# Two of the four weight sums of a seven-product pair: from VectorE to accumulating transfers issued by GpSimd

## The chip, the cores and the metric

The kernel runs on one core of one Trainium2 chip. The metric is the device time of one execution in microseconds. Before the change it is 2252.79 us, the median of three runs (2252.79 to 2252.91).

## What is computed

The reference is a trunk of two layers over 256 tokens of width 2048, all in float32. Each layer normalises its input, projects it by `w_in` (2048 x 6144), runs two kinds of attention, projects by `w_o` (2048 x 2048), adds the normalised result, and then runs a gated feed-forward block, which is where the change is:

```python
def swiglu(h, w_gate, w_up, w_down):
    return (jax.nn.silu(h @ w_gate) * (h @ w_up)) @ w_down
...
        h = rms_norm(x, pre_ffn_norm[l])
        f = swiglu(h, w_gate[l], w_up[l], w_down[l])
        x = x + rms_norm(f, post_ffn_norm[l])
```

`w_gate` and `w_up` are 2048 x 5632, `w_down` is 5632 x 2048.

## The kernel before

**Weights as a stream.** All weights are cut into blocks of 256 rows by 512 columns (512 KB), and `queue_pair` (line 96) lists the blocks in the order in which they are used. A block is held as a tile `raw` of 128 partitions by 2 by 512; the index 0 or 1 in the middle says which 128 rows. `fetch` (line 136) allocates the tile (four buffers) and issues its load on SyncE's queue (SP, line 140). `feed` (line 167) splits each block into two float32r parts: ScalarE makes `hi` (line 177), VectorE the rest `lo` (line 179), six buffers each. `weights(i, ahead)` (line 187) feeds the stream up to four blocks beyond the one that is asked for. TensorE forms each product as three matmuls: hi by hi, hi by lo, lo by hi.

**Gate and up.** A column chunk c (eleven per layer, 512 columns each) needs eight blocks of `w_gate` and eight of `w_up`, one of each per pair kp. Four PSUM banks collect the two token halves by gate and up. An ordinary pair (`eight`, line 726) makes eight products, 24 matmuls. The pairs kp 2, 4 and 6 (`SEVEN`; only 4 and 6 in a layer's first chunk, where the order is `FIRST_ORDER`) make seven products, 21 matmuls, by a Strassen-like scheme over the 2 x 2 blocks: token halves by row blocks, row blocks by gate or up (`seven`, line 736). It needs four sums of weight blocks. With g the gate block and u the up block they are t1 = g0 + u0, t3 = u0 + u1, t2 = t1 + u1 and t4 = t2 + g1. `mixed_weights` (line 145) makes them: four additions on VectorE (line 151) into two tiles T (t1 and t3 in one, t2 and t4 in the other), then the split of u1 (lines 155 and 156) and of the two T tiles into Th (ScalarE, line 160) and Tl (VectorE, line 162). The block g itself takes the ordinary split. There are 32 such pairs per layer, 64 in all. After the last pair of a chunk the extra products are combined in four tiles w (lines 778 to 783, tag `t2`), and lines 788 to 791 apply the gate.

**Order.** The program is traced in the order of the code. A scheduler then orders each engine's instructions by its own model of when they are ready, with the traced order as priority; each engine's queue then runs strictly in that order, and an instruction that waits holds up all behind it. Tiles with the same tag share a fixed number of buffers, and the first writer of a tile waits for the last reader of the buffer's former tile. At a few places the order is given by hand. One is `in_turn` (line 183), which holds a small load behind the latest block's load. Another is the end of the output projection (lines 676 to 687), where `feed` and `fetch` are called with explicit indices while ScalarE and VectorE keep the traced order; there the stream's index `idx + 4` is the first gate block of the layer.

Of the kernel before, what the change touches and what calls it, by code (L numbers as in the profile page):

```python
# [9 lines left out]
F32 = mybir.dt.float32  # L10
# [3 lines left out]
ALU = mybir.AluOpType  # L14
# [3 lines left out]
P = 128  # L18
# [7 lines left out]
CW = 512  # L26
# [25 lines left out]
def kernel(  # L52
# [21 lines left out]
    nc = tc.nc  # L74
# [19 lines left out]
    stream = []  # L94
# [8 lines left out]
    sevens = set()  # L103
# [29 lines left out]
    raws, loads = [], []  # L133
    fed = [0]

    def fetch(upto):
        while len(raws) < min(upto, len(stream)):
            i = len(raws)
            raw = wpool.tile([P, 2, CW], F32, tag="raw", bufs=4, name=f"raw{i}")
            loads.append(nc.sync.dma_start(raw, stream[i]))  # L140
            raws.append(raw)

    mix_pool = [None]

    def mixed_weights(i):

        g, u = raws[i - 1], raws[i]
        sums = [mix_pool[0].tile([P, 2, CW], F32, tag="T", bufs=2, name=f"T{i}_{j}") for j in range(2)]
        t1, t3, t2, t4 = sums[0][:, 0, :], sums[0][:, 1, :], sums[1][:, 0, :], sums[1][:, 1, :]
        for o, a, b in ((t1, g[:, 0, :], u[:, 0, :]), (t3, u[:, 0, :], u[:, 1, :]), (t2, t1, u[:, 1, :]), (t4, t2, g[:, 1, :])):  # L150
            nc.vector.tensor_tensor(out=o, in0=a, in1=b, op=ALU.add)  # L151
        parts = []
        hi = wpool.tile([P, 2, CW], F32R, tag="hi", bufs=6, name=f"hi{i}")
        lo = wpool.tile([P, 2, CW], F32R, tag="lo", bufs=6, name=f"lo{i}")
        nc.scalar.activation(hi[:, 1, :], u[:, 1, :], AF.Copy)
        nc.vector.tensor_tensor(out=lo[:, 1, :], in0=u[:, 1, :], in1=hi[:, 1, :].bitcast(F32), op=ALU.subtract)
        parts.append((hi[:, 1, :], lo[:, 1, :]))
        for j in range(2):
            th = mix_pool[0].tile([P, 2, CW], F32R, tag="Th", bufs=3, name=f"Th{i}_{j}")
            nc.scalar.activation(th, sums[j], AF.Copy)  # L160
            tl = mix_pool[0].tile([P, 2, CW], F32R, tag="Tl", bufs=3, name=f"Tl{i}_{j}")
            nc.vector.tensor_tensor(out=tl, in0=sums[j], in1=th.bitcast(F32), op=ALU.subtract)  # L162
            parts += [(th[:, k, :], tl[:, k, :]) for k in range(2)]
        b22, t1, t3, t2, t4 = parts
        return {"b22": b22, "t1": t1, "t2": t2, "t3": t3, "t4": t4}

    def feed(upto):
        fetch(upto)
        while fed[0] < min(upto, len(stream)):
            i = fed[0]  # L170
            raw = raws[i]
            if i in sevens:
                ready[i] = mixed_weights(i)
                fed[0] += 1
                continue
            hi = wpool.tile([P, 2, CW], F32R, tag="hi", bufs=6, name=f"hi{i}")
            nc.scalar.activation(hi, raw, AF.Copy)  # L177
            lo = wpool.tile([P, 2, CW], F32R, tag="lo", bufs=6, name=f"lo{i}")
            nc.vector.tensor_tensor(out=lo, in0=raw, in1=hi.bitcast(F32), op=ALU.subtract)  # L179
            ready[i] = (hi, lo)  # L180
            fed[0] += 1
# [27 lines left out]
    nc.sync.dma_start(rows0, pre_mix_norm.rearrange("l (k p) -> (l k) p", p=P))  # L209
    load_x(0, 0)  # L210
    fetch(1)
    load_x(1, 0)
    fetch(2)
    load_x(0, 1)
    fetch(3)
# [75 lines left out]
    def transposed(t, g0, tiles, cols=range(4)):  # L291
        for cg in cols:
            pb = bank(f"xT_ps{t}_{cg}")
            for j in range(4):
                k = cg * 4 + j
                nc.tensor.transpose(pb[:, j * P : (j + 1) * P], xs[t][:, k * P : (k + 1) * P], ident)
            for j in range(4):
                k = cg * 4 + j
                rounded = nc.scalar.activation(
                    tiles[k][:, 0, t * P : (t + 1) * P], pb[:, j * P : (j + 1) * P], AF.Copy, scale=gains[:, g0 + k : g0 + k + 1]  # L300
                )
            for j in range(4):
                k = cg * 4 + j
                rest = nc.vector.scalar_tensor_tensor(
                    out=tiles[k][:, 1, t * P : (t + 1) * P],
                    in0=pb[:, j * P : (j + 1) * P],
                    scalar=gains[:, g0 + k : g0 + k + 1],
                    in1=tiles[k][:, 0, t * P : (t + 1) * P].bitcast(F32),
                    op0=ALU.mult,
                    op1=ALU.subtract,  # L310
                )
        return rounded, rest
# [36 lines left out]
    def unit(accs, stat, i, kp, toks, first, last, ahead=LOOKAHEAD):  # L349
        hi, lo = weights(i, ahead)  # L350
        for kk in range(2):
            tick()
            k = 2 * kp + kk
            for t in toks:
                st = stat[k]
                sh, sl = st[:, 0, t * P : (t + 1) * P], st[:, 1, t * P : (t + 1) * P]
                a = accs[t]
                nc.tensor.matmul(a, sh, hi[:, kk, :], start=first and kk == 0, stop=False)  # L358
                nc.tensor.matmul(a, sh, lo[:, kk, :], start=False, stop=False)  # L359
                nc.tensor.matmul(a, sl, hi[:, kk, :], start=False, stop=last and kk == 1)  # L360


    def evac_chunk(pool, acc, mg, ssm, gpost, c, t, nm, mpool=None):
        junk = pool.tile([P, CW], F32, tag="t2", name=f"jm_{nm}_{t}_{c}")
        nc.scalar.activation(junk, acc, AF.Square, accum_out=ssm[t][:, c : c + 1])
        if c % 2 == 0:
            mg[t, c // 2] = (mpool or pool).tile([P, 2, CW], F32, tag="qk", bufs=4, name=f"mg_{nm}_{t}_{c}")
        m = mg[t, c // 2][:, c % 2, :]
        nc.vector.tensor_tensor(out=m, in0=acc, in1=gpost[:, c * CW : (c + 1) * CW], op=ALU.mult)

    def rescale(mg, ssm, t, nm, then=None):
        tot = small.tile([P, 2], F32, tag="tot", name=f"tot_{nm}_{t}")
        nc.vector.tensor_reduce(out=tot[:, 0:1], in_=ssm[t], axis=AX.X, op=ALU.add)
        rsqrt(tot[:, 1:2], tot[:, 0:1], 1.0 / D, f"{nm}_{t}_p")
        for c in range(4):
            sl = xs[t][:, c * CW : (c + 1) * CW]
            nc.vector.scalar_tensor_tensor(
                out=sl, in0=mg[t, c // 2][:, c % 2, :], scalar=tot[:, 1:2], in1=sl, op0=ALU.mult, op1=ALU.add
            )
            if then is not None:  # L380
                then(t, c)
# [266 lines left out]
    for l in range(L):  # L648

        pool = tc.alloc_tile_pool(name=f"att{l}", bufs=6, reuse_waits="tile")  # L650
# [25 lines left out]
        idx = plan[l]["o"][3, 4]  # L676
        with tc.manual_schedule(engines={mybir.EngineType.Activation, mybir.EngineType.DVE}):
            feed(idx + 6)
            for kp in range(4, 8):
                unit(accs, mix, idx + kp - 4, kp, (0,), False, kp == 7, 0)  # L680
            evac_chunk(pool, accs[0], mg, ssm, gpost, 3, 0, f"o{l}")
            rescale(mg, ssm, 0, f"o{l}")
            for kp in range(4, 8):
                feed(idx + 3 + kp)
                fetch(idx + 8 + kp)
                unit(accs, mix, idx + kp - 4, kp, (1,), False, kp == 7, 0)
                transposed(0, 32 + l * KT, xT, cols=(kp - 4,))
        with tc.high_priority(offset=URGENT):
# [3 lines left out]
        pool.release()  # L692


        pool = tc.alloc_tile_pool(name=f"ffn{l}", bufs=6, reuse_waits="tile")
        gu = tc.alloc_tile_pool(name=f"gu{l}", bufs=1, reuse_waits="tile")
        mix_pool[0] = gu
        act = []
# [213 lines left out]
```

## Time and profile before

| | |
|---|---|
| median of three runs | 2252.79 us |
| the profiled execution | 2252.42 us |
| its span, first to last instruction | 2250.7 us |
| granted TensorE clock, mean | 0.998 |
| bytes read from HBM | 417.68 MB, 187 GB/s over the span |
| DMA share of the SP queue | 58.2% of 16 engines |
| the gate and up stage of layer 0 and layer 1 | from about 408 and 1520 us, for about 466 and 472 us |

A profile is one execution. Busy time is the time in which an engine's instructions run; the share is against the span. PE is TensorE's matmuls, PEld its weight loads, DVE VectorE, ACT ScalarE, POOL GpSimd, SP SyncE. A wait row names the instruction that waited and what ended its wait, then the total in us, how often, and the longest. In a timeline row the first number is the start and the second the duration. DVE instructions of one kind overlap a little: their durations are longer than the distance from start to start, and a sum over many is better taken from the starts.

### The profile page before, as it was taken

The page shows a single profiled execution, that of the slowest core. Times are in us where ns is not written, and L with a number is a line of the kernel's source. Part 1 is how long each engine was busy: PE and PEld are TensorE (multiplying, and loading weights), DVE is VectorE, ACT ScalarE, POOL GpSimd, SP SyncE. Part 2 cuts the span into 40 slices and gives each one's busy share as a digit, 9 for nine tenths or more (in the row PEclk, how much of TensorE's full clock was granted, in tenths as well). Part 3 has the DMA queues.
Part 4 walks back from the last instruction along what each step waited for, and adds up shares of the span by engine and source line. Part 5 has one row for each costly group of instructions (what it writes and reads, how often), then busy time and mean ns, then how long its engine had stood idle before and what let it go on. Part 6 is the DMA issues. An engine that isn't in the chain of part 4 may idle for free.

```text
span 2250.7 us, 28018 instructions
## 1 busy us (share of the span) xinstructions
PE 2225.4 (99%) x10210; PEld 1833.5 (81%) x10210; DVE 1626.3 (72%) x2225; ACT 1222.4 (54%) x1834; POOL 37.6 (2%) x76
## 2 busy tenths in 40 slices
PE   8999999999999999999999999999999999999998
PEld 6888888788888888888887888887888888888886
DVE  6666555899989988555576665559998998975555
ACT  6545555665555546444465555546655555554443
POOL 1010000000000000000010000000000000000000
PEclk9999999999999999999999999999999999999999
DMA  7555555475665666556565555554666566565553
GB/s 238 180 169 163 163 182 184 127 229 187 204 206 188 199 209 208 189 188 204 171 195 175 162 167 161 186 186 141 205 200 209 190 199 205 190 218 192 191 198 135
DMA packets 216699, 421.62 MB, mean 187 GB/s; under 512 B 13200, under 2 KB 13808, under 8 KB 216048
## 3 DMA queue, kind: packets, MB, share of 16 engines
q1 hardware_dynamic: 216560, 419.83, 58.2%
q8 instruction: 80, 1.31, 0.2%
q14 instruction: 59, 0.48, 0.1%
HBM read 417.68 MB, written 2.10 MB: 187 GB/s over the span
## 4 chain that ended last, share of the span: by engine, by line
PE 92%; DVE 3%; ACT 2%; DMA 2%; issue 0%; POOL 0%; SPq 0%; DVEq 0%; ACTq 0%
PE c L722 10%; PE c L723 10%; PE c L724 10%; PE in L358 8%; PE in L360 7%; PE in L359 7%; PE dn L843 7%; PE dn L840 7%; PE dn L841 7%; PE o L360 2%; PE o L358 2%; PE o L359 2%; PE p L724 2%; PE p L723 2%; PE p L722 2%; DVE lo L179 1%
## 5 line engine op out<-in xcount | busy, mean ns | idle before, releaser
L179 DVE TENSOR_TENSOR lo<-raw,hi 128x1024 fp32r<-128x1024 f32 x720 | 873.6, 1227 | 329.8 <-ACT hi L177 324.5
L177 ACT ACTIVATE hi<-raw 128x1024 fp32r<-128x1024 f32 x720 | 749.5, 1056 | 469.1 <-PE in L360 166.5
L722 PE MATMUL c<-hi,xF 128*128 128x512 f32 x960 | 377.8, 394 | 2.0 <-DVE w L783 1.6
L724 PE MATMUL c<-hi,xF 128*128 128x512 f32 x960 | 374.2, 391 | 0.0
L723 PE MATMUL c<-lo,xF 128*128 128x512 f32 x960 | 373.6, 390 | 0.0
L840 PE MATMUL dn<-hi,jh 128*128 128x512 f32 x656 | 255.6, 390 | 0.0
L841 PE MATMUL dn<-lo,jh 128*128 128x512 f32 x656 | 255.2, 389 | 0.0
L722 PEld LDWEIGHTS c<-hi,xF 128*128 128x128 f32 x960 | 180.6, 188 | 39.1 <-DVE w L783 2.5
L724 PEld LDWEIGHTS c<-hi,xF 128*128 128x128 f32 x960 | 180.4, 188 | 37.8
L723 PEld LDWEIGHTS c<-lo,xF 128*128 128x128 f32 x960 | 180.5, 188 | 36.3
L843 PE MATMUL dn<-hi,jl 128*128 128x512 f32 x656 | 202.1, 389 | 0.0
L160 ACT ACTIVATE Th<-T 128x1024 fp32r<-128x1024 f32 x128 | 135.2, 1056 | 116.9 <-DVE T L151 106.5
L822 DVE TENSOR_TENSOR jl<-act,jh 128x512 fp32r<-128x512 f32 x88 | 60.7, 692 | 161.6 <-ACT jh L820 159.3
L820 ACT ACTIVATE jh<-act 128x512 fp32r<-128x512 f32 x88 | 55.0, 631 | 219.3 <-PE dn L841 213.5
L162 DVE TENSOR_TENSOR Tl<-T,Th 128x1024 fp32r<-128x1024 f32 x128 | 156.2, 1220 | 1.0 <-ACT Th L160 0.3
L358 PE MATMUL in<-hi,xT 128*128 128x512 f32 x384 | 155.3, 405 | 1.3 <-ACT hi L177 1.3
L358 PE MATMUL in<-hi,xI 128*128 128x512 f32 x384 | 154.0, 401 | 0.0
L359 PE MATMUL in<-lo,xT 128*128 128x512 f32 x384 | 150.7, 392 | 0.6 <-DVE lo L179 0.6
L360 PE MATMUL in<-hi,xT 128*128 128x512 f32 x384 | 150.8, 393 | 0.0
L359 PE MATMUL in<-lo,xI 128*128 128x512 f32 x384 | 149.9, 390 | 0.3 <-DVE lo L179 0.3
L360 PE MATMUL in<-hi,xI 128*128 128x512 f32 x384 | 150.2, 391 | 0.0
L841 PEld LDWEIGHTS dn<-lo,jh 128*128 128x128 f32 x656 | 123.1, 188 | 25.6
(247 smaller groups left out, 3224.0 us busy)
## 6 DMA issues: line engine op xcount, KB each, us to landing
raw<-in_w_in_dram SPq DMA_DIRECT2D x192, 512.0 KB, 3.8
raw<-in_w_gate_dram SPq DMA_DIRECT2D x176, 512.0 KB, 3.9
raw<-in_w_up_dram SPq DMA_DIRECT2D x176, 512.0 KB, 4.5
raw<-in_w_down_dram SPq DMA_DIRECT2D x176, 512.0 KB, 4.3
raw<-in_w_o_dram SPq DMA_DIRECT2D x64, 512.0 KB, 4.1
x<-in_x_dram SPq DMA_DIRECT2D x4, 512.0 KB, 7.6
gpost_mix<-in_post_mix_norm_dram SPq DMA_DIRECT2D x2, 1024.0 KB, 7.8
gpost_ffn<-in_post_ffn_norm_dram SPq DMA_DIRECT2D x2, 1024.0 KB, 7.2
```

Source lines behind the costliest of these rows:

```text
L162: nc.vector.tensor_tensor(out=tl, in0=sums[j], in1=th.bitcast(F32), op=ALU.subtract)
L177: nc.scalar.activation(hi, raw, AF.Copy)
L179: nc.vector.tensor_tensor(out=lo, in0=raw, in1=hi.bitcast(F32), op=ALU.subtract)
L358: nc.tensor.matmul(a, sh, hi[:, kk, :], start=first and kk == 0, stop=False)
L359: nc.tensor.matmul(a, sh, lo[:, kk, :], start=False, stop=False)
L360: nc.tensor.matmul(a, sl, hi[:, kk, :], start=False, stop=last and kk == 1)
L722: nc.tensor.matmul(a, sh, hi, start=first, stop=False)
L723: nc.tensor.matmul(a, sh, lo, start=False, stop=False)
L724: nc.tensor.matmul(a, sl, hi, start=False, stop=last)
L840: nc.tensor.matmul(accs[c, t], sh, hi[:, kk, :], start=first, stop=False)
L841: nc.tensor.matmul(accs[c, t], sh, lo[:, kk, :], start=False, stop=False)
L843: nc.tensor.matmul(accs[c, t], sl, hi[:, kk, :], start=False, stop=last)
```

## The change

For the up block of a seven-product pair `fetch` loads only the half u1 into `raw`. A new helper allocates a tile Ta (two buffers), copies g0 and u1 from HBM into its halves by two more loads on SP's queue, and then issues on GpSimd's queue one transfer that reads u0 twice and adds it to both halves in SBUF. Ta then holds t1 and t3. `mixed_weights` takes Ta in place of its first T tile and adds only t2 and t4 on VectorE; T has one buffer instead of two. To make room, the feed-forward pool's tiles of tag `t2` get five buffers instead of six. The clamp on `fetch` at the end of the output projection keeps the first seven-product pair's block from being fetched before the pool that holds Ta exists.

```diff
@@ fetch
-            loads.append(nc.sync.dma_start(raw, stream[i]))
+            if i in sevens:
+                loads.append(nc.sync.dma_start(raw[:, 1, :], stream[i][:, 1, :]))
+                add_in_memory(i)
+            else:
+                loads.append(nc.sync.dma_start(raw, stream[i]))
             raws.append(raw)
 
     mix_pool = [None]
 
+    added = {}
+
+    def add_in_memory(i):
+
+        t = mix_pool[0].tile([P, 2, CW], F32, tag="Ta", bufs=2, name=f"Ta{i}")
+        nc.sync.dma_start(t[:, 0, :], stream[i - 1][:, 0, :])
+        nc.sync.dma_start(t[:, 1, :], stream[i][:, 1, :])
+        nc.gpsimd.dma_start(t, stream[i][:, 0:1, :].to_broadcast([P, 2, CW]), accum_op=ALU.add)
+        added[i] = t
+
     def mixed_weights(i):
 
         g, u = raws[i - 1], raws[i]
-        sums = [mix_pool[0].tile([P, 2, CW], F32, tag="T", bufs=2, name=f"T{i}_{j}") for j in range(2)]
+        sums = [added[i], mix_pool[0].tile([P, 2, CW], F32, tag="T", bufs=1, name=f"T{i}")]
         t1, t3, t2, t4 = sums[0][:, 0, :], sums[0][:, 1, :], sums[1][:, 0, :], sums[1][:, 1, :]
-        for o, a, b in ((t1, g[:, 0, :], u[:, 0, :]), (t3, u[:, 0, :], u[:, 1, :]), (t2, t1, u[:, 1, :]), (t4, t2, g[:, 1, :])):
+        for o, a, b in ((t2, t1, u[:, 1, :]), (t4, t2, g[:, 1, :])):
             nc.vector.tensor_tensor(out=o, in0=a, in1=b, op=ALU.add)
@@ the end of the output projection
-                fetch(idx + 8 + kp)
+                fetch(min(idx + 8 + kp, idx + 12))
@@ the feed-forward stage
-        pool = tc.alloc_tile_pool(name=f"ffn{l}", bufs=6, reuse_waits="tile")
+        pool = tc.alloc_tile_pool(name=f"ffn{l}", bufs=5, reuse_waits="tile")
```

## Prediction

> **What bounds the kernel now.** I read the engine line of the page first, then windows over the gate/up stage, then PE's waits and the chain of waits inside it.
>
> ```profile
> PE 2225.4 (99%) x10210; PEld 1833.5 (81%) x10210; DVE 1626.3 (72%) x2225; ACT 1222.4 (54%) x1834; POOL 37.6 (2%) x76
> ```
> ```profile
> 408.00:470.00 62.00, 57.73 (x260) 45.89 (x259) 57.35 (x121) 43.74 (x88) 0.00 (x0) 0.97 0.50 153
> 470.00:875.00 405.00, 405.00 (x1827) 335.59 (x1825) 362.93 (x425) 225.68 (x260) 0.00 (x0) 1.00 0.62 201
> 1520.00:1590.00 70.00, 66.45 (x299) 52.73 (x299) 65.14 (x136) 48.69 (x97) 0.00 (x0) 0.98 0.45 142
> 1590.00:1992.00 402.00, 402.00 (x1810) 332.97 (x1809) 357.78 (x418) 223.42 (x256) 0.00 (x0) 1.00 0.63 203
> ```
> ```profile
> 492.00:534.00 42.00, 42.00 (x191) 34.81 (x190) 40.47 (x47) 24.22 (x28) 0.00 (x0) 1.00 0.66 218
> ```
>
> The columns are the stretch, its length, busy time of PE, PEld, DVE, ACT and POOL, the granted clock, the DMA share and GB/s. PE has no idle microsecond in the 405 and 402 us that hold nearly all seven-product pairs. One column chunk (191 PE instructions: five eight-product pairs of 24 matmuls, three seven-product pairs of 21, eight transposes) takes 42.0 us. DVE is busy but is not what ends last. Only where a layer's gate/up stage begins does PE stand idle: 62.00 - 57.73 = 4.3 us in layer 0 and 70.00 - 66.45 = 3.6 us in layer 1. Work taken from VectorE can be repaid in those 7.9 us only; a loss has no such cap.
>
> ```profile
> PE p L723 <- DVE lo L179: 1.8, 1, 1.8
> PE q L722 <- ACT Th L160: 1.1, 1, 1.1
> PE c L722 <- DVE w L783: 0.8, 1, 0.8
> ```
> ```profile
> 429.55 4.92 DMA raw<-in_w_up_dram
> ...
> 439.40 1.20 DVE T L151 x2
> ...
> 442.48 4.02 DMA raw<-in_w_gate_dram
> ...
> 448.82 1.89 DVE T L151 x3
> ...
> 456.52 4.95 DMA raw<-in_w_up_dram
> ```
>
> These are PE's waits in 408 to 470 us (total, times, longest) and the chain there (start, length). The chain alternates between weight loads of 4 to 5 us and weight sums of 0.6 us each. Sums stand before two of the three waits (Th, and the w of line 783), not before the one for the gate pair's lo.
>
> **The sums that go.** Two of four sums per pair leave VectorE.
>
> ```profile
> L151 DVE TENSOR_TENSOR T<-raw,raw 128x512 f32<-128x512 f32 x64 | 44.2, 691 | 8.7 <-DMA raw<-in_w_up_dram 6.7
> L151 DVE TENSOR_TENSOR T<-raw 128x512 f32<-128x512 f32 x64 | 43.9, 685 | 0.0
> ```
>
> That is 88.1 us of DVE's 1626. In steady chunks it buys nothing, since PE is full there. The first chunk of a layer has two such pairs, so four sums, which follow each other at 0.60 us (below), leave its chain: at most 2.4 us a layer, 4.8 us in all.
>
> **The transfers that come.** Per pair the SP queue loses half of the up load (256 KB) and gets two copies of 256 KB; POOL gets one accumulating transfer that reads 256 KB twice and adds it into 512 KB of SBUF. No row of before shows an accumulating transfer or a DMA issued by POOL. The nearest rows:
>
> ```profile
> raw<-in_w_up_dram SPq DMA_DIRECT2D x176, 512.0 KB, 4.5
> ...
> gpost_ffn<-in_post_ffn_norm_dram SPq DMA_DIRECT2D x2, 1024.0 KB, 7.2
> out_dram<-x SPq DMA_DIRECT2D x8, 256.0 KB, 2.3
> ```
>
> The two copies should land in between 2.3 us (256 KB) and 4.5 us (512 KB); nearest is 4.5, the same bytes. The accumulate moves 512 KB and reads its destination besides: from 4.5 us (as a plain load) to 7.2 us (twice the bytes). I take 6, in the middle. From free buffer to finished sum that is 2.3 + 4.5 = 6.8 at the low end, 4.5 + 7.2 = 11.7 at the high end, 10.5 taken; the second copy's issue on SP (0.37 us, row below) and POOL's own issue, for which no row exists and which I put at the same 0.37, make it 11.2, and 7.5 to 12.4 at the ends. POOL is idle in these stages, so nothing queues behind its waits.
>
> **Who waits for the new sum.** The rows are one steady chunk, on DVE, then SP, then PE.
>
> ```profile
> 672.77 0.69 DVE L151 TENSOR_TENSOR T<-raw,raw 128x512 f32<-128x512 f32 x1
> 673.38 0.68 DVE L788 TENSOR_TENSOR w<-c,w 128x512 f32<-128x512 f32 x1
> ...
> 678.29 0.69 DVE L151 TENSOR_TENSOR T<-raw 128x512 f32<-128x512 f32 x1
> 678.89 0.69 DVE L151 TENSOR_TENSOR T<-T,raw 128x512 f32<-128x512 f32 x1
> 679.49 0.69 DVE L156 TENSOR_TENSOR lo<-raw,hi 128x512 fp32r<-128x512 f32 x1
> 680.09 0.69 DVE L151 TENSOR_TENSOR T<-T,raw 128x512 f32<-128x512 f32 x1
> 680.69 1.22 DVE L162 TENSOR_TENSOR Tl<-T,Th 128x1024 fp32r<-128x1024 f32 x1
> 681.83 1.22 DVE L179 TENSOR_TENSOR lo<-raw,hi 128x1024 fp32r<-128x1024 f32 x1
> ...
> 685.44 0.69 DVE L151 TENSOR_TENSOR T<-raw,raw 128x512 f32<-128x512 f32 x1
> ...
> 695.61 1.42 DVE L151 TENSOR_TENSOR T<-T,raw 128x512 f32<-128x512 f32 x2
> ```
> ```profile
> 680.81 0.37 SPq L140 DMA_DIRECT2D raw<-in_w_up_dram  x1
> ```
> ```profile
> 688.28 0.39 PE L722 MATMUL q<-Th,sh 128*128 128x512 f32 x1
> ...
> 698.48 0.39 PE L722 MATMUL q<-Th,sh 128*128 128x512 f32 x1
> ```
>
> The pairs are kp 2 (sums 672.77 to 680.7), kp 4 (from 685.44) and kp 6 (t2 at 695.61). After the change DVE's add for t2 waits for the accumulate, and behind it in DVE's queue stand the lo splits of the next weights, for which PE waits in the end. Cover: PE takes the first kp 2 sum at 688.28, its Tl ended at 680.69 + 1.22 = 681.9, so 6.4 us of lead.
>
> The wait's length depends on **where SP has the two copies**. Of the two Ta buffers, the one for kp 6 is that of kp 2, free when kp 2's Tl ends: 681.9. Its sum is needed at 695.61. That leaves 13.7 us, or 11.3 if DVE, four sums lighter by then, is 2.4 us earlier; my 11.2 just fits, and 12.4 would cost DVE 1.1 us out of the lead. Kp 2 and kp 4 have longer: their buffers are those of the chunk before. This holds if the copies are issued when their buffer is free and not in the traced order, behind the half load of line 140, which waits for its own buffer. Two rows speak for it: the sum at 672.77 runs ahead of line 788, which is traced before it, and
>
> ```profile
> 0.97 0.20 POOL L246 MEMSET negones<- 128x128 f32 x1
> ```
>
> runs at 0.97 us though it is traced behind a whole column chunk. What is ready early is put early in its queue. So I cost the copies and the accumulate at nothing in steady chunks.
>
> **The DMA engines** are the other cover. At a share of 0.62 the 405 us hold 405 / 42 = 9.6 chunks of 16 loads, so a 512 KB load takes 0.62 x 405 / 154 = 1.63 us of all engines. A chunk after the change has 16 - 3 x 0.5 + 3 x 1 = 17.5 such units and three accumulates of a units each. With a = 1 that is 33.4 us of the 42.0, with a = 2 38.3, with a = 3 43.2. I take 2, one read more per byte written, so the engines are 91% busy and loads will land later than now.
>
> The Trainium skill, Collectives: The Full Stack, section "The bandwidth ceiling: the fold count and why AG ≠ RS ≠ AR", says that an add in the transfer path goes at about half the rate of a copy, because it reads two sources; no run here shows one yet, and by it a would be 1.9 and the chunk's DMA work 38.0 us. The Trainium skill, DMA: Bandwidth & Descriptors, section "Anatomy of one DMA — SWDGE (gpsimd) path", puts a GpSimd transfer at 2.0 us and its bytes at 436 GB/s, an estimate of 3.2 us for 512 KB where I take 6; the sum would be the same, since both fit.
>
> **Small parts.** T keeps one buffer: its next writer (t2 of kp 4, after 685.44) comes after kp 2's second Tl (about 683 to 684.2). Five t2 buffers instead of six: the four w of a chunk are 42 us apart from the next four. The clamped fetch shortens only the traced order; loads wait for their four buffers in any case. All three at 0; without that cover each is one 0.6 to 1.2 us wait per pair or chunk.
>
> **Sum.** The profiled execution took 2252.42 us (span 2250.7 and 1.7 around it), 0.37 below the median of 2252.79. Steady chunks: 0. Each layer's start: 0 to -2.4 from the sums, against later loads on the same chain; I take -0.7 net. 2252.42 - 1.4 = **2251.0 us**. From the full gain of 4.8 to equal loss, its own range is 2247.6 to 2257. A measurement of this kernel can tell about 0.2%, 4.5 us.
>
> **Rivals.**
> *Contention at 91% share (slower).* Two pairs at a layer's start bring 2 x (0.5 + 2) = 5 units, 8.2 us of DMA work, onto a chain with three load waits (4.92, 4.02, 4.95). Half of it there is +4 a layer, all of it +8: 2252.4 + 8 to 16. Steady chunks lose too if every landing grows by one accumulate (3.3 us), which is half of the 6.4 us lead: decisive once twice that falls on one pair. About 2265, up to 2290. Against it: the share is only 0.50 at the start.
> *Copies behind the half load (slower).* Then the sum comes L = 4.6 (680.81 to 685.44) + 6 + 0.7 for issues = 11.3 us after the up buffer is free. A turn from kp 2 to kp 4 is L + 1.8 (t2, t4, half lo) against PE's 698.48 - 688.28 = 10.2; from kp 6 to the next chunk's kp 2 it is L + 1.8 + six splits of 1.14 (680.69 to 681.83) = L + 8.6. Together 3L + 12.2 against 42.0: it decides from L = 9.9; at 11.3 a chunk takes 46.1, and 20 chunks cost 82: 2334. Up to L = 12.5: 2408. Against it: the early issues above.
> *DMA bound (slower).* From a = 2.8. With a = 3, 20 x 1.2 = 24 us: 2276; with a = 4, 48.1 a chunk: 2374. Nothing in before shows a.
> *Faster.* The whole 4.8 us and no later loads: 2247.6, just past the bound. For it: sums before two of three waits. Against: 1.1 + 0.8 us of those waits per layer.
>
> **Chances.** Hidden 0.46, contention 0.24, copies behind 0.12, DMA bound 0.12, faster by over 0.2% 0.06. So same 0.46, slower 0.48. The likeliest single case is the first, 2251.0. The range 2248 to 2340 takes in it, contention, the lower half of "DMA bound" and of "copies behind"; some 0.17 stays outside.
>
> **What would show it.** Right: DVE about 88 us lighter, PE at 42.0 us a chunk with no waits in 470 to 875, the Ta copies issued more than 10 us before their t2 add, a DMA share near 0.9 there, the accumulate landing in 4.5 to 7.2 us. Wrong: DVE's t2 adds waiting on the accumulate for microseconds, Ta issues right behind their half load, a share of 1, or PE's waits at the layer starts above 4.3 and 3.6 us.

## The result and the profile after

| | before | after |
|---|---|---|
| median, 11 runs each on one chip | 2252.79 us (2250.37 to 2253.2) | 2259.23 us (2255.61 to 2265.07) |
| ratio, 95% interval | | 1.0029 (1.0021 to 1.0037) |
| the profiled execution, its span | 2252.42, 2250.7 us | 2265.07, 2263.2 us |

The kernel became slower by 0.29%, 6.4 us between the medians. The profiled execution after is the longest of its eleven, so its trace shows the loss enlarged: 12.65 us against the profiled execution before.

The page after, engines, queues and DMA issues:

```profile
PE 2230.4 (99%) x10210; PEld 1834.3 (81%) x10210; DVE 1553.1 (69%) x2097; ACT 1224.2 (54%) x1834; POOL 115.5 (5%) x140
...
q0 software_dynamic: 17408, 33.56, 8.6%
...
L156 POOL DMA_DIRECT2D Ta<-in_w_up_dram x64 | 77.9, 1218 | 1347.7 <-DVE ssx_ffn L337 284.6
...
raw<-in_w_up_dram SPq DMA_DIRECT2D x112, 512.0 KB, 5.7
Ta<-in_w_up_dram POOLq DMA_DIRECT2D x64, 512.0 KB, 8.2
...
Ta<-in_w_gate_dram SPq DMA_DIRECT2D x64, 256.0 KB, 4.1
```

VectorE has 128 instructions less and is 73.2 us lighter. The accumulating transfer lands 8.2 us behind its issue in the median, and POOL is busy 1.22 us with each issue. A plain load of an up block now lands in 5.7 us instead of 4.5.

PE's waits over the whole execution, the rows of the gate and up stages (total, times, longest), after:

```profile
PE c L736 <- DVE w L797: 6.4, 4, 2.9
...
PE p L736 <- ACT Th L174: 2.3, 2, 1.3
PE c L736 <- ACT hi L191: 2.3, 3, 1.7
```

The first row was, before,

```profile
PE c L722 <- DVE w L783: 1.6, 2, 0.8
```

and it is now the largest of the stages. The windows (same columns as in the prediction) say where:

```profile
408.00:450.00 42.00, 38.13 (x169) 29.77 (x169) 38.23 (x98) 29.35 (x73) 2.68 (x3) 0.96 0.60 167
...
450.00:470.00 20.00, 18.00 (x77) 13.99 (x76) 13.87 (x17) 11.99 (x13) 1.10 (x1) 1.00 0.80 241
470.00:492.00 22.00, 22.00 (x103) 18.06 (x102) 17.25 (x20) 10.57 (x12) 2.42 (x2) 1.00 0.92 251
492.00:515.00 23.00, 21.20 (x90) 17.01 (x89) 18.34 (x21) 11.87 (x14) 2.42 (x2) 0.96 0.92 275
...
550.00:875.00 325.00, 325.00 (x1466) 269.14 (x1465) 264.01 (x297) 181.81 (x208) 26.78 (x22) 1.00 0.87 254
```

From 550 us on PE has no idle microsecond, with the DMA engines 87% busy: the steady chunks hide everything. PE stands idle for 3.9 us in 408 to 450 us, 2.0 in 450 to 470 and 1.8 in 492 to 515. Up to 470 us that is 5.9 against 4.3 before; the last is new. The DMA share in 450 to 515 us is 0.80 to 0.92.

A ruler for this is the start of one matmul, the first q product by Th of kp 6 (the pair whose PE work ends a chunk's seven-product pairs). From one chunk to the next it measures a **turn**. On PE's timeline before, chunks one to three of layer 0:

```profile
453.10 0.39 PE L722 MATMUL q<-Th,sh 128*128 128x512 f32 x1
...
496.61 0.39 PE L722 MATMUL q<-Th,sh 128*128 128x512 f32 x1
...
539.02 0.39 PE L722 MATMUL q<-Th,sh 128*128 128x512 f32 x1
```

and after, chunks one to four:

```profile
454.33 0.39 PE L736 MATMUL q<-Th,sh 128*128 128x512 f32 x1
...
499.66 0.39 PE L736 MATMUL q<-Th,sh 128*128 128x512 f32 x1
...
545.87 0.39 PE L736 MATMUL q<-Th,sh 128*128 128x512 f32 x1
...
588.32 0.39 PE L736 MATMUL q<-Th,sh 128*128 128x512 f32 x1
```

Before, the turns are 43.5 and then 42.4; after, 45.3, 46.2 and then 42.4, to the end of the layer. In layer 1 they are 43.6 and 42.4 before, 46.4, 47.2 and then 42.4 after. The excess is 1.8 + 3.8 + 2.8 + 4.8 = 13.2 us, all of the 12.65. **Four turns hold the loss**, two at each layer's beginning. The landings in the trace say the same: in both layers the last transfer of the first chunk, the three of the second and the first of the third are used 0.02 to 0.15 us after they land, so something stands and waits for each. From then on every transfer lands 1.25 us or more ahead of its first use.

What stands in the second of the four, on the timelines of SP, POOL, ScalarE and VectorE:

```profile
449.89 1.21 POOL L156 DMA_DIRECT2D Ta<-in_w_up_dram  x1 [9.88 <-DVE T L165]
...
474.95 1.23 DVE L176 TENSOR_TENSOR Tl<-Ta,Th 128x1024 fp32r<-128x1024 f32 x1
...
476.20 0.34 SPq L154 DMA_DIRECT2D Ta<-in_w_gate_dram  x1
...
477.76 0.47 SPq L155 DMA_DIRECT2D Ta<-in_w_up_dram  x1
...
484.01 1.21 POOL L156 DMA_DIRECT2D Ta<-in_w_up_dram  x1 [11.90 <-DVE Tl L176]
...
494.10 0.69 DVE L165 TENSOR_TENSOR T<-Ta,raw 128x512 f32<-128x512 f32 x1 [6.27 <-DMA Ta<-in_w_up_dram]
494.17 1.06 ACT L174 ACTIVATE Th<-Ta 128x1024 fp32r<-128x1024 f32 x1 [8.02 <-DMA Ta<-in_w_up_dram]
494.35 1.21 POOL L156 DMA_DIRECT2D Ta<-in_w_up_dram  x1 [9.12 <-issue]
```

The first row is the transfer of kp 2 of the second chunk, issued 4.4 us before PE's kp 6 of the first (454.33). The second is the Tl that reads it; the last is already the transfer of the third chunk's kp 2. The rows between are kp 6 of the second chunk. Its buffer is free when kp 2's Tl ends (476.18); SP issues the first copy 0.02 us later, so the copies are hoisted (put ahead of work that is traced before them) as forecast. But the sum can start only at 494.10: **17.9 us** from free buffer to usable transfer. VectorE and ScalarE both stand in line for it, 6.3 and 8.0 us. The last row is put down to issue, but 6.1 of its 9.12 us are its own two copies, which land until 491.35; it then starts 0.3 us after kp 6's transfer has landed (494.02).

### The profile page after: what moved, and what is told of

It is laid out like the page before. It is cut to its first block, busy times and chain, and to the rows that moved or that the text cites. A ratio compares the mean times of both kernels' runs of the same rounds, so it can differ in the third digit from the quotient of the medians.

```text
span 2263.2 us, 28439 instructions
## 1 busy us (share of the span) xinstructions
PE 2230.4 (99%) x10210; PEld 1834.3 (81%) x10210; DVE 1553.1 (69%) x2097; ACT 1224.2 (54%) x1834; POOL 115.5 (5%) x140
## 3 DMA queue, kind: packets, MB, share of 16 engines
q0 software_dynamic: 17408, 33.56, 8.6%
## 4 chain that ended last, share of the span: by engine, by line
PE 88%; DMA 4%; DVE 3%; ACT 3%; issue 1%; POOL 0%; DVEq 0%; SPq 0%; ACTq 0%; POOLq 0%
PE c L736 9%; PE c L737 9%; PE c L738 9%; PE in L372 7%; PE in L374 7%; PE in L373 7%; PE dn L854 7%; PE dn L857 7%; PE dn L855 7%; PE o L374 2%; PE o L372 2%; PE o L373 2%; DMA Ta<-in_w_up_dram 2%; PE p L736 2%; PE p L738 2%; PE p L737 2%
## 5 line engine op out<-in xcount | busy, mean ns | idle before, releaser
L156 POOL DMA_DIRECT2D Ta<-in_w_up_dram x64 | 77.9, 1218 | 1347.7 <-DVE ssx_ffn L337 284.6
L857 PEld LDWEIGHTS dn<-hi,jl 128*128 128x128 f32 x656 | 123.1, 188 | 25.7
```

The source lines that it names most:

```text
L156: nc.gpsimd.dma_start(t, stream[i][:, 0:1, :].to_broadcast([P, 2, CW]), accum_op=ALU.add)
L857: nc.tensor.matmul(accs[c, t], sl, hi[:, kk, :], start=False, stop=last)
```

## The experiments

All but the control of the w tiles start from the changed kernel. Unless an edit says otherwise the time is a median of 6 to 11 runs; before measured 2251.7 to 2252.3 us beside them. The changes of place use one edit, with a condition that says which pairs get transfers; the others make all four sums on VectorE again, with t1 and t3 in a tile of tag Ta:

```diff
+                    if CONDITION:
+                        dma_sums.add(lay["up"][c, kp])
...
-            if i in sevens:
+            if i in dma_sums:
                 loads.append(nc.sync.dma_start(raw[:, 1, :], stream[i][:, 1, :]))
                 add_in_memory(i)
```

**The small parts alone** (CONDITION: `False`).

> All four sums on VectorE again, and only the small parts of the change are left: five t2 buffers, one T buffer beside two Ta buffers (VectorE writes t1 and t3 into Ta), the clamped fetch. Theory A (the loss arises in the first chunks of a layer, where the new transfers land late on the chain of waits): no transfer is new here, so 2252.8 as before, within 1.5 us. Rival B (the accumulating transfers cost a little in every chunk): also 2252.8. Rival C (fewer buffers and the clamp hold up the first chunks, since PE's largest waits after the change end with the w of line 797): about 2259.

Measured 2251.62 us, ratio 0.9999 (0.999 to 1.0008). The clamp, one T buffer and five t2 buffers cost nothing.

**Only late chunks** (`c >= 3`), and **only the first three** (`c < 3`).

> Accumulating transfers from the fourth chunk of a layer on (c 3 to 10), VectorE sums in c 0 to 2. Theory A: the steady chunks hide them, so 2252.8 within 1.5 us, no PE wait between the fourth chunk and the end of the stage, DMA share there near 0.89. Rival B: 48 of 64 pairs keep them, so 48/64 of the 6.4 us stay: 2257.6. Rival C: 2259.

> The complement: accumulating transfers in c 0 to 2 alone, VectorE sums in c 3 to 10. Theory A: the whole loss stays, 2258 to 2261, with PE waits at the layer starts as after the change (about 7.5 us of PE idle per layer) and a granted clock of 0.96 in the stretch that follows the later stall. Rival B: 16 of 64 pairs, 2254.4. Rival C: 2259 too, so this run alone does not part A from C; the first one does.

Measured 2257.2 us, 1.0022 (1.0014 to 1.0031), and 2255.17 us, 1.0014 (1.0005 to 1.0023). The first three chunks alone lose 3.0 us, not the whole 6.4, so the theory that only they count fell. The loss is not bound to a layer's start: with the late chunks it appears where the transfers begin. Turns of this version in layer 0: 43.3, 42.4, **44.6**, then 42.4. VectorE's and POOL's timelines at this place:

```profile
543.25 1.23 DVE L181 TENSOR_TENSOR Tl<-Ta,Th 128x1024 fp32r<-128x1024 f32 x1 [8.81 <-ACT Th L179]
```
```profile
531.60 1.33 POOL L159 DMA_DIRECT2D Ta<-in_w_up_dram  x1 [388.43 <-PE c L743]
542.27 1.24 POOL L159 DMA_DIRECT2D Ta<-in_w_up_dram  x1 [9.35 <-issue]
```

VectorE stands 8.8 us behind the first transfer's Th. The second transfer's copies have landed at 532.65, yet it is issued at 542.27, 0.3 us after the first has landed (542.01). The long turns of the profiled execution show about 2 us per layer (44.2 in layer 1), some 4 of the 5 lost in all; the rest isn't in a row that I could name.

**No addition in the transfer.**

```diff
-        nc.gpsimd.dma_start(t, stream[i][:, 0:1, :].to_broadcast([P, 2, CW]), accum_op=ALU.add)
+        nc.gpsimd.dma_start(t, stream[i][:, 0:1, :].to_broadcast([P, 2, CW]))
```

> GpSimd's transfer copies instead of adding, so t1 and t3 hold u0 alone (the two additions are left out); bytes from HBM, descriptors, queue and waits stay. Theory A1 (what is late is the add itself, which reads its destination too): the transfer takes about half of the 16 engines' time, 1.6 us instead of 3.1, lands in about 5 us instead of 8.2, and the loss shrinks to 0 to 3 us: 2253 to 2256. Rival A2 (what is late is the 768 KB more per pair on shared engines and the chain of copy, wait and transfer, not the add): landing stays over 7 us and the time at 2258 to 2260.

Measured 2247.73 us, 0.998 (0.9971 to 0.9989). From its page:

```profile
q0 software_dynamic: 9216, 33.56, 4.3%
...
Ta<-in_w_up_dram POOLq DMA_DIRECT2D x64, 512.0 KB, 5.8
```

The same transfers in number, size and place, without the addition: they take half the DMA time and about half the packets (9216 against 17408), land in 5.8 us instead of 8.2, and the loss turns into a gain of 4.5 us, more than either expectation had. Copies, queues and order by themselves lose nothing; the loss needs the addition.

**Only the first chunk** (`c == 0`, 4 of 64 pairs), and **only the last three** (`c >= 8`, 18 pairs).

> Accumulating transfers in the first chunk of a layer only (4 of 64 pairs). Theory D (each onset costs once: the first turn or two after the transfers begin lag by 2 to 7 us, then every chunk takes 42.41 us again): the first chunk keeps the gain that the run with three chunks showed there (its kp 6 came 38.8 us after the chunk's first matmul against 42.0 before) and no second chunk pays for it, so 2246 to 2250, faster than before. Rival B (a cost per transfer): 4/64 of 6.4 us, 2252.6. Rival E (the first chunk's gain is only borrowed, and the turn to the second chunk gives it back in any case because the loads of the next weights were pushed behind): 2252 to 2254.

> Accumulating transfers in the last three chunks of a layer only (c 8 to 10, 18 of 64 pairs). Theory D: one onset per layer as with c 3 to 10, which measured +5.0: 2255 to 2258, and one turn of 44 to 45 us per layer at the onset among turns of 42.4. Rival B: 18/64 of 6.4, 2254.0, no turn longer than 42.6.

Measured 2248.98 us, 0.9986 (0.9977 to 0.9995), and 2256.87 us, 1.002 (1.0011 to 1.0029). Eighteen pairs lose as much as forty-eight (2257.2): no cost per transfer fits. The four pairs of the first chunks gain 3.2 us: this is where the forecast saw sums on the chain, and no second chunk of transfers follows. VectorE of the late version stands again where the transfers begin:

```profile
755.26 1.22 DVE L181 TENSOR_TENSOR Tl<-Ta,Th 128x1024 fp32r<-128x1024 f32 x1 [9.42 <-ACT Th L179]
```

**The w tiles first**, on the changed kernel and, as a control, on the kernel before.

```diff
+                    with tc.high_priority(offset=URGENT):
-                    nc.scalar.copy(w[0], p1)
+                        nc.scalar.copy(w[0], p1)
...
```

> The changed kernel, with the five instructions of lines 793 to 797 (the w tiles that free the four extra PSUM banks) given a higher scheduling priority, so that they stand earlier in VectorE's and ScalarE's queues. Theory F (PE stalls in the first turns because the next chunk's banks are those of the extra products, and their release stands in VectorE's queue behind an instruction that waits for a late transfer): the waits for w of lines 794 to 797 go, 2252 to 2256. Rival G (the turns are long because the weights themselves come late; the banks are only what shows): PE waits as long, now for hi, lo or Th, 2257 to 2261.

> The kernel before with the same higher priority for those five instructions, as a control. Theory F: before has 0.8 us of waits for w per layer, so -1 to -2 us: 2250.5 to 2252. Rival G: 2252.2 within 1 us. If the reordering itself does harm, over 2253, and the previous run is then read against this one.

Measured 2257.73 us, 1.0028 (1.0016 to 1.0039), and 2251.15 us, 0.9996 (0.9987 to 1.0004). PE's waits for the w of line 797 are gone, but a wait for a later w has their size:

```profile
PE actT_ps L812 <- DVE w L806: 5.5, 2, 2.9
```

The w wait is only where the delay comes out. The turns of the first are 47.8 and then 42.4 in layer 0, 46.8 and 42.4 in layer 1: how the loss divides between a layer's two long turns differs from one profiled execution to the next.

**Every other chunk** (`c % 2 == 1`, 30 pairs).

> Transfers only in the odd chunks of a layer (chunks 1, 3, 5, 7, 9: 30 of the 64 pairs), four sums on VectorE in the others. Question: is the loss paid once per layer, or each time that transfers begin behind a chunk without them? Once per layer (a phase that stays shifted): turns of 42.4 us after the first one, total +4 to +6 against before, about 2257. At each beginning (the plain chunk gives VectorE its lead's shape back): 5 turns per layer of about 44.4 instead of 42.4, 10 x 2 = +20, about 2272. By cost per transfer (30 of 64 of +6.5): +3, about 2255.

Measured 2282.5 us (4 runs), 1.0133 (1.0117 to 1.0148): +30 us. Turns of layer 0: 49.6, 42.4, 47.4, 42.4, 44.3, 42.4, 43.4, 42.4, 43.6, 42.5. A loss comes each time that transfers begin behind a chunk without them; the price differs, from 0.6 to 7 us in the ten places of the two layers.

**One transfer per chunk** (`kp == 4`, 22 pairs).

> Transfers only for the pair kp 4 of every chunk (22 of the 64 pairs, the first chunk's among them), four sums on VectorE for kp 2 and kp 6. If the loss comes from the second chunk's three transfers standing close together behind the loads (a path of 17.9 us where 11.2 was assumed), one transfer per chunk has a whole chunk for its path: no turn above 42.6, and half of the first chunk's gain, 2250 to 2252. If any transfer that begins in a full pipeline costs a turn, the second chunk's turn is 44 to 46 again: 2256 to 2258.

Measured **2246.6 us**, 0.9974 (0.9965 to 0.9983), the fastest version. Its page and windows:

```profile
Ta<-in_w_up_dram POOLq DMA_DIRECT2D x22, 512.0 KB, 6.1
```
```profile
450.00:492.00 42.00, 42.00 (x188) 34.16 (x188) 39.34 (x46) 27.48 (x31) 1.24 (x1) 1.00 0.78 244
492.00:534.00 42.00, 42.00 (x191) 34.81 (x190) 36.45 (x44) 22.92 (x27) 1.21 (x1) 1.00 0.66 207
```

No PE idle in the second chunk, the clock at 1.00, a landing of 6.1 us, and turns of 42.9 and then 42.4 (43.7 and 42.4 in layer 1, as before). With one transfer per chunk, beginning in the first, no turn is lost. The gain of 5.7 us is more than the half of the first chunk's gain that was expected; the account of the prediction comes back to it.

**Two transfers per chunk**: kp 2 and kp 4 (`kp != 6`), and kp 2 and kp 6 (`kp != 4`).

> Transfers for kp 2 and kp 4 of every chunk (only kp 4 in a layer's first chunk): 42 of the 64 pairs. The transfers of kp 6, whose buffer is the one that kp 2 of the same chunk gives back last, are left out. If that short turn of a buffer makes the loss: no long turn at the second chunk, 2246 to 2251. If more than one transfer per chunk at the onset is too many: turns of 44 to 47 at the second chunk, 2256 to 2260.

> Transfers for kp 2 and kp 6 (only kp 6 in a layer's first chunk): 42 of the 64 pairs, as many as with kp 2 and kp 4, and the same bytes. If the short turn of the buffer from kp 2 to kp 6 makes the loss: turns of 44 to 47 at the second chunk and 2256 to 2260, against 2246 to 2251 for kp 2 and kp 4. If the number per chunk makes it, the two come out alike, within 0.2%.

Measured 2315.2 us (5 runs), 1.0283 (1.0269 to 1.0297), and 2307.36 us (4 runs), 1.0248 (1.0234 to 1.0262). Both expectations fell: the loss is spread over nearly all chunks, not at the beginning, and some ten times as large. The queues of the second, in one steady chunk:

```profile
602.71 0.68 DVE L170 TENSOR_TENSOR T<-Ta,raw 128x512 f32<-128x512 f32 x1
...
613.50 0.37 SPq L147 DMA_DIRECT2D raw<-in_w_up_dram  x1
613.92 0.46 SPq L157 DMA_DIRECT2D Ta<-in_w_gate_dram  x1
...
620.55 1.21 POOL L159 DMA_DIRECT2D Ta<-in_w_up_dram  x1 [33.79 <-ACT Th L179]
...
630.15 0.69 DVE L170 TENSOR_TENSOR T<-Ta,raw 128x512 f32<-128x512 f32 x1 [6.45 <-DMA Ta<-in_w_up_dram]
...
630.40 1.22 POOL L159 DMA_DIRECT2D Ta<-in_w_up_dram  x1 [8.64 <-issue]
```

The buffer for kp 6 is free at 603.4, when kp 2's t2 add has read it, but its first copy is issued at 613.92, right behind a raw load that waits for its own buffer. In this program the scheduler has put the copies there. It is the prediction's second rival, "copies behind the half load", in another kernel: a stand of 6.5 us here, and of 7.0 on average in seven chunks. The transfer of the last row is held besides: its copies have landed at 621.92, but it starts 0.3 us after the one before it has landed (630.08). So these two say what a late place of the copies in SP's queue costs, with the transfers then close behind each other, and nothing on which pair makes the loss of the changed kernel, or on whether two transfers per chunk are too many.

**Where VectorE and ScalarE use the transfer.** If standing in line makes the loss, the splits that wait behind can be sent ahead. The first edit does so for kp 6 of the second chunk and VectorE alone, the second for all pairs from the second chunk on; the third and fourth for both engines, at kp 6, and at kp 2 and kp 6, of the second chunk.

```diff
+            if i in late:
+                held.append(i)
+                fed[0] += 1
+                continue
             if i in sevens:
...
+            if held and i >= held[0] + 2:
+                with tc.issue_after(last.ins), tc.issue_after(split.ins):
+                    ready[held[0]] = mixed_weights(held[0])
+                held.pop()
```

(`last` is VectorE's lo, `split` ScalarE's hi; the first two have no `split`.)

> All transfers as in the changed kernel. Only for kp 6 of each layer's second chunk, the sums and splits that read the transfer's result are put behind the lo splits of the next two blocks (kp 7's gate and up) in VectorE's queue. In the changed kernel VectorE stands 6.3 us at this place with these splits queued behind. If the loss is VectorE standing in order behind a late transfer: the 46.2 and 47.2 us turns fall to 42.4 to 44, and the time to 2252 to 2256. If the late landing itself or the loads beside it make the loss, whatever the order: turns stay at 45 to 47, and 2258 to 2261.

> The same order for every seven-product pair from the second chunk on. If standing in order is the loss and the later sums still come in time for TensorE: the time of the kernel with the second chunk alone or a little less, 2250 to 2256. If the sums then come too late (they are 2 to 4 us ahead of TensorE in steady chunks of the changed kernel, and two splits are 2.3 us): every chunk loses 1 to 3 us, 2270 to 2310.

> As the kernel with the sums of kp 6 of the second chunk put behind kp 7's splits, but on ScalarE's queue too: Th also stands behind the hi parts of kp 7. With VectorE's order alone, VectorE no longer stood at the sum but 6.5 us at kp 7's lo, for which ScalarE's hi stood behind Th. If in-order standing behind the late transfer on both engines makes the loss of the second turn: no stand over 3 us there, the turn at 42.4 to 43 in both layers, and 2253 to 2257. If not: turns of 44 to 47 again and 2258 to 2261.

> The same for kp 2 and kp 6 of the second chunk. If the first turn (45 to 48 us) is also a stand, behind kp 2's transfer: it falls to 43 to 44, and 2250 to 2254. If kp 2's sums then come too late for TensorE, whose lead there is small: the first turn stays at 45 to 48 or grows, 2256 to 2262.

Measured 2258.51 (1.0029, 1.0017 to 1.004), 2351.19 (5 runs; 1.0429, 1.0415 to 1.0444), 2257.77 (1.0025, 1.0016 to 1.0034) and 2257.27 us (1.0026, 1.0015 to 1.0036). **The theory of the stand falls** as the cause by itself: the time stays. The second turn is shorter than in the changed kernel (44.7 and 45.0 in the third version against 46.2 and 47.2), but that shows little, since with the w tiles first it was 42.4 and the kernel took as long (2257.73 us). With both queues reordered, ScalarE and VectorE stand for something else instead:

```profile
491.73 1.06 ACT L198 ACTIVATE hi<-raw 128x1024 fp32r<-128x1024 f32 x1 [6.24 <-DMA raw<-in_w_gate_dram]
...
492.82 2.52 DVE L200 TENSOR_TENSOR lo<-raw,hi 128x1024 fp32r<-128x1024 f32 x2 [6.07 <-ACT hi L198]
```

The next weight block isn't there either. In these rows what comes late in the second chunk is the data, transfers and loads alike. The version with all pairs (+99 us) shows that steady chunks have no room for later sums.

**The transfer in two halves**, one for t1 and one for t3 (10 runs).

```diff
-        nc.gpsimd.dma_start(t, stream[i][:, 0:1, :].to_broadcast([P, 2, CW]), accum_op=ALU.add)
+        for j in range(2):
+            nc.gpsimd.dma_start(t[:, j, :], stream[i][:, 0, :], accum_op=ALU.add)
```

> The accumulating transfer of each pair is issued as two of half the size, one for t1 and one for t3. Nothing in the program makes the second wait for the first. If GpSimd issues one accumulating transfer only when the one before it has landed: the second halves are issued 4 to 6 us behind the first ones, an idle time put down to issue, and the pair's path is longer, 2262 to 2285. If several can be under way: 1.2 to 1.5 us behind, the first half lands earlier than the whole did, 2256 to 2262.

Measured 2250.94 us, 1.0001 (0.9992 to 1.001): the loss is gone in the median, with the same bytes and additions; neither expectation had that. (Its profiled execution is the longest of its ten, 2256.98 us, and still has turns of 46.3 us in layer 0 and three of 44.3 to 44.4 in layer 1.) POOL's timeline in the second chunk:

```profile
477.91 0.87 POOL L157 DMA_DIRECT2D Ta<-in_w_up_dram  x1 [9.03 <-ACT hi L170]
479.61 0.86 POOL L157 DMA_DIRECT2D Ta<-in_w_up_dram  x1 [0.83 <-DMA Ta<-in_w_up_dram]
489.43 1.77 POOL L157 DMA_DIRECT2D Ta<-in_w_up_dram  x2 [8.96 <-ACT Th L175]
```

The two of the last row are issued 0.5 us apart (489.43 and 489.97), so two halves can be under way at once, though never three are in this trace. Whole transfers never are: in all the versions that have them, none is issued before the one ahead of it has landed. In 51 places its own copies had landed earlier, by 1.2 to 10.2 us, and there it follows 0.3 us after that landing. That is what stands behind the waits put down to issue. It can't be the whole loss: with the w tiles first, and with both engines reordered at kp 2 and kp 6, no transfer is held in this way, and the loss is there. The first half no longer waits for both copies. Kp 6's sum starts 15.0 us behind its free buffer (472.9 to 487.87) instead of 17.9, and its wait then ends on a raw load, while ScalarE still stands 6.4 us for the second half.

## Why the prediction was wrong

*Right, with wrong sizes: steady chunks.* PE at full, turns of 42.4 us, copies issued when their buffer is free (for kp 6 of the fifth chunk at 597.46, 20.0 us ahead of its t2 add at 617.47), a DMA share of 0.87 there. But the path from free buffer to landing is 12.5 us or more in every chunk from the fourth on, above the 12.4 of the high end; kp 6 takes 13.0 to 13.9. It is hidden because kp 6 has 17.8 to 19.2 us there and not 11.3 to 13.7. The tightest pair is kp 2, of which the prediction says that it has longer: 14.3 to 16.4 us, and only 1.25 to spare at the worst. The right outcome is luck in part. The value of a was right: 8.6% of 2263.2 us over 64 transfers is 3.04 us of all engines each, against 4.3% of 2246.0 over 64, 1.51, for the plain copy of the same size: a = 2.0. The Trainium skill, Collectives: The Full Stack, section "The bandwidth ceiling: the fold count and why AG ≠ RS ≠ AR", has ReduceScatter, whose add reads two sources, at about half the rate of AllGather, which copies; the two kernels here agree, 3.04 against 1.51 us.

*Right: the small parts.* They cost nothing.

*Right in size only: the gain.* The full gain was put at 4.8 us, for the four sums of each layer's start; without the addition it is 4.5. But the kernel with one transfer per chunk gains 5.7 and takes only two of these four sums away. Its granted clock in 408 to 450 us and in 1520 to 1562 us is 1.00, where before has 0.96; by an estimate that is 0.04 x 42 = 1.7 us a layer. So how much of a gain is VectorE's relief isn't shown.

*Mis-sized: VectorE's relief.* 73.2 us instead of 88: the 128 durations overlap, as the text before the prediction warns; at 0.60 us a step it would have been 77.

*Mis-sized: the path of one transfer.* "I take 6, in the middle" measured 8.2 in the median and 10.0 at the place that counts; 6.0 holds only where transfers are few (6.0 in the first-chunk version, 6.1 with one per chunk). POOL's issue was "the same 0.37" and is 1.2. The copies landed 5.2 us (477.76 to 482.99) after the last issue where 4.5 was taken, and the transfer began 1.0 us later. "Nothing queues behind its waits" doesn't hold for POOL either: the next transfer does, 3.0 us in the row at 494.35 and up to 10.2 in other versions. The path was put at 11.2 us with 12.4 as its high end, against 11.3 to 13.7 available, and measured 17.9 at kp 6 of the second chunk. The landing and the copies were priced from rows of before, with a steady share of 0.62, although the same text forecast 0.91.

*The step that failed: "Steady chunks: 0", counted from a layer's second chunk on.* The Sum gave a layer 0 to -2.4 us at its start, -0.7 net, and nothing behind it. It came to +3.2 per layer, half of the 6.4 us between the medians. The start itself isn't what failed: transfers in the first chunks alone gain 3.2 us over both layers. The loss lies in the turns into and out of the second chunk, which the prediction counted among its 20 steady ones, with a path of 11.2 us that "just fits". The hoisting that covers the steady chunks brings the next chunk's copies and accumulates forward into the first one and its turn (kp 2's transfer at 449.89), the DMA share is then 0.80 to 0.92, and kp 6's path takes 17.9 us. The forecast was decided by the row of the wrong chunk.

The contention rival had the sign and nearly the size (2260 to 2268 against 2259.23), and was set at 0.24 because "the share is only 0.50 at the start". That was the share of the first chunk before the change. But the size is luck: the rival has the loss made by the two pairs of a layer's first chunk, and these alone gain.

*Open.* That the loss comes where transfers begin, and that it needs the addition, is shown; so is that three transfers per chunk lose where one doesn't. Not shown is how the loss divides between the transfer's own late landing, the loads that it delays and the transfers that wait for the one ahead, and why halves of the same bytes do so much better. Whether two per chunk lose by themselves isn't known, since those two versions place the copies differently. Three Ta buffers, the other way to start the path earlier, weren't tried.

## What to carry to other kernels

Before you move an engine's additions into transfers, price the transfer at the DMA share that the kernel will have with it, and at twice the DMA time of a copy; then compare its whole path (buffer free, copies, issue, landing) with the room in the first chunk that has it, not in a steady one. A pipeline that hides everything once it runs can still lose a few us each time that a heavier feed begins, so look at the turns one by one. Thin the change out before you drop it: one transfer per chunk gained (0.9974) where all of them lost.

## What the hardware showed that I had not expected

- An accumulating transfer of 512 KB lands in 6.0 to 6.1 us in the median where few are under way and in 8.2 us (up to 10.0 in the rows shown) where the DMA engines are near 0.9; the same transfer without the addition in 5.8 us at the same places, with the engines at 0.77. The Trainium skill, DMA: Bandwidth & Descriptors, section "Anatomy of one DMA — SWDGE (gpsimd) path", gives 2.0 us and the bytes at 436 GB/s, an estimate of 3.2 us; the median of every run here is above it.
- Issuing it holds POOL 1.22 us; the halves together hold it 113.1 us for 128, 0.88 us each.
- A whole accumulating transfer of 512 KB was never issued before the one ahead of it had landed, in 14 traces; two halves of 256 KB were under way at once. What makes the difference isn't shown.
- A stall of PE has no fixed price in granted clock here. The clock is 0.96 in 492 to 515 us after, with 1.8 us of PE idle, and 1.00 in 450 to 470, with 2.0. In 408 to 450 it is 0.96 after and 1.00 in the kernel with one transfer per chunk, with 3.9 and 3.4 us of idle.
